# Four edits to the small matmuls of a hybrid mLSTM and sparse-attention layer on one core: compression operands laid out by offset, a zero-padded gather, and broadcasts in another form

## The chip, the core and the metric

One core of one Trainium2 chip runs the whole layer in one launch. The metric is the device time of that launch in microseconds (us). The engines are TensorE (PE in the rows, with PEld for its weight loads), VectorE (DVE), ScalarE (ACT), GpSimd (POOL) and SyncE (SP), which issues the DMAs. Each engine works through its own instructions in order, and semaphores tie the engines together.

## The reference, cut to what matters

```python
D_MODEL, SEQ = 2048, 512
def reference(x, c, ...):
    mod = silu(c) @ w_ada + b_ada
    shift, scale, gate = split(mod, 3)
    h = rmsnorm(x, ln_g) * (1 + scale) + shift
    p = h @ w_in + b_in                      # one projection, split into 15 parts
    y_m = mlstm_group(...)                   # 4 heads of 256, chunked recurrence, gated by rows i and f
    y_n = nsa_group(...)                     # 16 query heads in 4 groups: compressed, selected and window attention
    y = concat([y_m, y_n]) @ w_out
    return rmsnorm(x + gate * y, final_g)
...
    # inside nsa_group: 31 blocks of 32 positions, at a stride of 16
    def compress(a, pos, w1, w2):
        blk = a[:, cidx] + pos
        return gelu(blk.reshape(..., CMP_LEN * dh) @ w1) @ w2
    k_cmp, v_cmp = compress(kc, ...), compress(vc, ...)
    p_c = masked_softmax(q @ k_cmp - slopes * distance)
    o_c = p_c @ v_cmp                        # the compressed branch, one of three that are gated and added
```

All tensors are float32. A product that has to keep that precision is made in one of two ways here: a plain float32 matmul, which the trace shows as two MATMUL records, or a split of an operand into a high and a low part in fp32r (hi/lo), with one record for each product of parts.

## The kernel before

The work is tiled to 128 partitions with the 512 positions along the free dimension. It runs through these stages.

Lines 155 to 277 normalise x, transpose it, compute shift and scale (`gemv`, float32 matmuls with 32 columns of weights at four column positions of the array, L203) and project the first seven column tiles (L256). Every later projection is `proj` (L279): two weight tiles of 128x1024 come by SP from DRAM into three rotating buffers (`raw`, L113), `split` (L119) makes a high part on ACT and a low part (names ending in `l`, L126) on DVE or POOL, and 48 matmuls of 512 columns add up one tile (L291 to L293). In the attention stage all low parts are made on POOL (L797).

Lines 345 to 413 compute the gate rows of the mLSTM. `gr` holds the projected rows, `fl` and `mr` are the results of two scans, and `rw` = `fl - mr` has four rows, one for each head. In each `memory_head` (L668) a matmul broadcasts one of these rows to 128 partitions: `rb` (L709), float32, four partitions deep, 512 columns.

`block_rows` (L418) writes the compression operand `cst` from a projection in PSUM. `compress` (L437) multiplies it with `w1`: 16 float32 matmuls of 124 columns for keys and 16 for values (`hid`, L444), each of which reads every eighth element of `cst`. The value result ends in `vcmp`, 32 partitions deep.

`attend` (L499) runs for 4 groups and 4 blocks of 128 queries. Its `gather` (L539) transposes the weights of four heads on PE, takes a high part on ACT (`ph`) and a low part on DVE (`pl`), and adds two matmuls of 512 columns into `o` (L548, L549). For the compressed branch these are 32 partitions deep (`phc`, `plc` with `vcmp`); for the others 128.

`gate_columns` (L778) runs as side work between the weight tiles of the mLSTM projections: 64 DMAs and 64 DVE operations make `gacc`, and 16 float32 matmuls of one column (`gcps`, L793) reduce it over partitions to the columns `gcol`. In the output stage `chunk_rows` (L833) broadcasts `gcol` into rows with 16 float32 matmuls of 128 columns (`gps`, L838); the products of the output projection are `po` (L899 to L901, and L908 to L910 for the last chunk).

The order on each engine comes from a scheduler that simulates the program, so a change of one operation can move others.

Of the kernel before, what the change touches and what calls it, by code (L numbers as in the profile page):

```python
# [86 lines left out]
def layer_kernel(ctx: ExitStack, tc: tile.TileContext, x, cols, ada, ada_g, w_ko, w_tiles,  # L87
# [221 lines left out]
    gr = const.tile([P, T], F32, name="gr")  # L309
    kcmp = const.tile([P, NG, 32], F32, name="kcmp")  # L310
    vcmp = const.tile([32, NG, P], F32R, name="vcmp")
# [14 lines left out]
    na = napool.__enter__()  # L326

# [54 lines left out]
    rw = gr[64:68, :]  # L382
# [10 lines left out]
    ve.tensor_sub(rw, fl, mr)  # L393
# [17 lines left out]
    for hd in range(MH):  # L411
# [5 lines left out]
            .rearrange("p (g t) -> p g t", g=NG) for vr in range(2)] for kv in range(2)]  # L417
    def block_rows(kv, ct2):  # L418
        nm = f"{'kv'[kv]}c{ct2}"
        ps = proj(nm)  # L420
        for gg in range(2):
            r = slice(64 * gg, 64 * gg + 64)
            pv = ps[r, :].rearrange("p (b l r) -> p b l r", l=8, r=2)
            for par in range(2):
                for vr in range(2):
                    po = COLS["pos"][0] + ((kv * 2 + par) * 2 + vr) * 8
                    ve.scalar_tensor_tensor(
                        cst[kv][vr][64 * par:64 * par + 64, 2 * ct2 + gg, :]
                        .rearrange("p (b l) -> p b l", l=8),
                        pv[:, :, :, par], bcol(nm)[r, :],  # L430
                        ct[r, po:po + 8].unsqueeze(1).to_broadcast([64, 32, 8]),
                        op0=ALU.add, op1=ALU.add)
# [3 lines left out]
                   zero[0:32, 0:1].to_broadcast([32, NG * P]))  # L436
    def compress(kv):  # L437

        hid = psb("ms", f"hid{kv}")
# [59 lines left out]
    def attend(g, qs, kh, kl, vt):  # L499
# [6 lines left out]
        for i in reversed(range(NT)):  # L506
# [161 lines left out]
    def memory_head(hd, vh, vl):  # L668
# [39 lines left out]
        dc = COLS["delta"][0] + hd * 16  # L708
        pe.matmul(rb, ct[64:68, dc:dc + 1].to_broadcast([4, P]), rw, start=True, stop=True)  # L709
# [68 lines left out]
    def gate_columns():  # L778
        for n in range(4):
            acc = na.tile([P, T], F32, tag="q", name=f"gacc{n}", bufs=QB)  # L780
            for k in range(KT):
# [12 lines left out]
            ve.tensor_add(gcol[:, 4 * n:4 * n + 4], ps[:, 0:4], col("b_agate", 4 * n, 4))  # L794
# [37 lines left out]
    wl_l = op.tile([P, KT, 256], F32R, name="wl_l")  # L832
    def chunk_rows(n, c0, cn):  # L833
# [195 lines left out]
```

## Time and profile before

| | |
|---|---|
| three timed runs | 1137.73, 1138.68 (median), 1139.94 us |
| the profiled execution | 1138.83 us, with a span of 1137.0 us |
| granted TensorE clock, mean | 0.996 |
| PE busy in the span | 1110.3 us, 98% |
| DVE, ACT, POOL busy | 668.1, 546.6 and 198.3 us |

The span runs from the first to the last instruction, and the 1.8 us around it are launch and end. A timeline row shows when an instruction starts and how long it is in flight. PE matmuls overlap, so what a matmul costs PE is the distance from its start to the next start, not its length.

### The profile page before, as it was taken

What the parts mean: (1) busy time and instruction counts of PE and PEld (TensorE: products, weight loads), DVE (VectorE), ACT (ScalarE), POOL (GpSimd) and SP (SyncE); (2) the same over time, 40 slices, a digit from 0 to 9 for tenths busy, and PEclk for the clock granted to TensorE, in tenths of its full rate; (3) what the DMA queues carried; (4) which work ended last, traced back from release to release, by engine and by line L of the source; (5) the groups of instructions that cost most, each with busy time, mean ns of one, the idle gap of its engine ahead of it and who ended that gap; (6) DMA issues with size and microseconds to landing.
All of it is one profiled execution on the core that took longest, in us unless ns stands there. A gap on an engine that the chain in (4) does not pass through costs nothing.

```text
span 1137.0 us, 18337 instructions
## 1 busy us (share of the span) xinstructions
PE 1110.3 (98%) x6796; PEld 919.1 (81%) x6796; DVE 668.1 (59%) x1712; ACT 546.6 (48%) x1222; POOL 198.3 (17%) x174
## 2 busy tenths in 40 slices
PE   4999999999999999999999999999999999999997
PEld 4777788887887888788788777888888888888896
DVE  5766464216647657666666885578567357334273
ACT  5443452237666758766756734333433354223242
POOL 1000200443335325333533210000000000000000
PEclk9999999999999999999999999999999999999999
DMA  9999423232111211121121442238416222444334
GB/s 378 406 402 363 146 93 130 93 112 74 56 56 59 72 56 56 62 68 57 61 70 57 138 158 77 91 134 290 151 57 214 84 91 75 148 140 133 104 114 158
DMA packets 49338, 150.29 MB, mean 132 GB/s; under 512 B 5856, under 2 KB 7776, under 8 KB 48736
## 3 DMA queue, kind: packets, MB, share of 16 engines
q1 hardware_dynamic: 49248, 149.12, 37.7%
q8 instruction: 53, 0.87, 0.3%
q14 instruction: 37, 0.30, 0.1%
HBM read 144.90 MB, written 4.19 MB: 131 GB/s over the span
## 4 chain that ended last, share of the span: by engine, by line
PE 93%; DVE 2%; DMA 2%; ACT 1%; issue 0%; POOL 0%; SPq 0%; ACTq 0%; POOLq 0%; DVEq 0%
PE ko L256 7%; PE po L899 5%; PE po L900 5%; PE po L901 5%; PE pj_q L291 3%; PE pj_mz L291 3%; PE pj_mx L291 3%; PE pj_mz L292 3%; PE pj_mv L291 3%; PE pj_q L292 3%; PE pj_mz L293 3%; PE pj_q L293 3%; PE pj_mx L292 3%; PE pj_mv L293 3%; PE pj_mv L292 3%; PE pj_mx L293 3%
## 5 line engine op out<-in xcount | busy, mean ns | idle before, releaser
L524 ACT ACTIVATE ep<-ep,nm 128x512 f32<-128x512 f32 (+3 forms) x128 | 71.3, 558 | 19.3 <-DVE nm L517 18.6
L749 POOL TENSOR_TENSOR sm<-sm,mhalf 128x1 f32<-128x1 f32 x16 | 10.1, 640 | 254.5 <-DVE sm L748 113.1
L788 DVE SCALAR_TENSOR_TENSOR gacc<-adag,sil,gacc 128x512 f32<-128x512 f32 x60 | 48.0, 801 | 7.5 <-DMA adag<-in_dram 6.9
L517 DVE CUSTOM_DVE_ANT_0 ep<-ss,bias 128x512 f32<-128x512 f32 (+3 forms) x64 | 30.3, 486 | 30.7 <-PE tps L543 22.1
L517 DVE CUSTOM_DVE_ANT_0 ep<-sw,bias 128x512 f32<-128x512 f32 (+3 forms) x64 | 29.9, 484 | 18.9 <-PE sw L585 12.9
L194 DVE SCALAR_TENSOR_TENSOR acc<-ada,sil,acc 128x256 f32<-128x256 f32 x75 | 35.7, 476 | 1.5
L220 ACT ACTIVATE hhi<-xts,md 128x512 fp32r<-128x512 f32 x16 | 13.1, 817 | 47.3 <-DVE md L210 47.3
L537 DVE TENSOR_SCALAR ep<-ep,ff 128x512 f32<-128x512 f32 (+3 forms) x80 | 33.2, 461 | 0.6
L861 POOL TENSOR_TENSOR rf<-rf,mhalf 128x1 f32<-128x1 f32 x4 | 2.2, 549 | 178.7 <-ACT tz L854 163.1
L547 DVE TENSOR_TENSOR pls<-tps,phs 128x512 fp32r<-128x512 f32 x40 | 27.0, 685 | 10.6 <-ACT phs L546 10.1
L547 DVE TENSOR_TENSOR plw<-tpw,phw 128x512 fp32r<-128x512 f32 x40 | 27.2, 684 | 6.7 <-ACT phw L546 6.1
L504 POOL TENSOR_SCALAR bias<-ct 128x640 f32<-128x640 f32 x16 | 29.4, 1839 | 2.3 <-DVE nm L517 1.2
L546 ACT CAST phw<-tpw 128x512 fp32r<-128x512 f32 x40 | 22.8, 583 | 13.3 <-PE tpw L543 8.4
L524 ACT ACTIVATE ec<-ec,nm 128x32 f32<-128x32 f32 x64 | 20.3, 317 | 17.6 <-DVE nm L517 17.2
L546 ACT CAST phs<-tps 128x512 fp32r<-128x512 f32 x40 | 23.0, 582 | 11.2 <-DVE nm L517 5.0
L203 PEld LDWEIGHTS gp<-ada,cb 128*32 128x32 f32 x1328 | 20.5, 112 | 8.9 <-issue 6.8
L543 PE MATMUL tpw<-ct,ep 128*128 128x128 f32 x160 | 26.8, 273 | 0.1
L517 DVE CUSTOM_DVE_ANT_0 ec<-ss,bias 128x32 f32<-128x32 f32 x48 | 8.9, 187 | 29.1 <-PE ss L575 28.8
L535 ACT ACTIVATE ep<-ep,ff 128x512 f32<-128x512 f32 (+3 forms) x48 | 23.5, 552 | 4.4 <-DVE ff L529 4.3
L232 PE MATMUL xt<-ct,xs 128*128 128x128 f32 x64 | 11.0, 330 | 14.3 <-DVE xs L169 12.4
L203 PE MATMUL gp<-ada,cb 128*32 128x64 f32 x1328 | 24.9, 224 | 0.0
L543 PE MATMUL tps<-ct,ep 128*128 128x128 f32 x160 | 24.8, 272 | 0.0
(1084 smaller groups left out, 3831.4 us busy)
## 6 DMA issues: line engine op xcount, KB each, us to landing
ada<-in_dram SPq DMA_DIRECT2D x64, 512.0 KB, 7.0
adag<-in_dram SPq DMA_DIRECT2D x64, 256.0 KB, 3.7
wo<-in_dram SPq DMA_DIRECT2D x32, 512.0 KB, 3.4
w_q<-in_dram SPq DMA_DIRECT2D x16, 512.0 KB, 3.5
w_mx<-in_dram SPq DMA_DIRECT2D x16, 512.0 KB, 3.4
w_mv<-in_dram SPq DMA_DIRECT2D x16, 512.0 KB, 3.4
w_mz<-in_dram SPq DMA_DIRECT2D x16, 512.0 KB, 3.5
w_mo<-in_dram SPq DMA_DIRECT2D x16, 512.0 KB, 3.4
```

The lines of the kernel that those rows point to most:

```text
L256: pe.matmul(ko_ps[j], (wl if p == 1 else wh)[:, c], (hlo if p == 2 else hhi)[k], start=(k == 0 and p == 0), stop=(k == KT - 1 and p == 2))
L291: pe.matmul(ps, wh[:, c], hhi[k], start=(k == 0), stop=False)
L292: pe.matmul(ps, wh[:, c], hlo[k], start=False, stop=False)
L293: pe.matmul(ps, wl[:, c], hhi[k], start=False, stop=(k == KT - 1))
L517: ve.tensor_tensor_reduce(dst, src, bs, -0.125, 3.0e38, ALU.add, ALU.min, nm[:, c:c + 1])
L524: sc.activation(tiles[hd], tiles[hd], AF.Exp, bias=nm[:, 4 * br + hd:4 * br + hd + 1], scale=-1.0, accum_out=zz[:, 4 * br + hd:4 * br + hd ...
L543: pe.transpose(tp[0:rows, hd * P:(hd + 1) * P], srcs[hd], ident)
L547: ve.tensor_sub(pl[0:rows, :], tp[0:rows, :], ph[0:rows, :].bitcast(F32))
L788: ve.scalar_tensor_tensor(acc, raw, w, acc, op0=ALU.mult, op1=ALU.add)
L899: pe.matmul(pss[i][:, :cn], yh[k][:, t], wh[:, c], start=f0, stop=False)
L900: pe.matmul(pss[i][:, :cn], yh[k][:, t], wl[:, c], start=False, stop=False)
L901: pe.matmul(pss[i][:, :cn], yl[k][:, t], wh[:, c], start=False, stop=l0)
```

## The change

There are five edits.

1. `cst` is laid out with the offset `l` first, so that `hid` reads 127 elements in a row (the columns between groups are computed and not used) in place of 4 x 31 elements at a stride of eight. `block_rows` writes with the inverse stride.
2. `vcmp` and the compressed `ph` become 128 partitions deep: high part in rows 0 to 31, low part in rows 32 to 63, zeros below, which POOL writes by a memset in every gather. One matmul takes the place of two.
3. `rw` becomes an fp32r tile of 128 partitions with high rows, low rows and zeros, and `dsel` a selector of the same depth; `rb` is one fp32r matmul. To build them there are new operations on DVE, ACT and POOL and three small DMAs on SP.
4. `gcps` uses 32 columns of ones as weights at four column positions, with 128 columns of `gacc` moving, and a DVE transpose follows.
5. `gps` is made from `gcol` in high and low parts: DVE multiplies the identity with them into `dg`, and two fp32r matmuls per chunk add the two.

```diff
-    gr = const.tile([P, T], F32, name="gr")
+    rw = const.tile([P, T], F32R, name="rw")
+    dsel = const.tile([P, 64], F32R, name="dsel")
-    vcmp = const.tile([32, NG, P], F32R, name="vcmp")
+    vcmp = const.tile([P, NG, P], F32R, name="vcmp")
...
-    ve.tensor_sub(rw, fl, mr)
+    gp.memset(rs, 0.0)
+    gp.memset(ds, 0.0)
+    for r in range(2):
+        nc.sync.dma_start(ds[4 * r:4 * r + 4, :], cols[0:4, COLS["delta"][0]:COLS["delta"][0] + 64])
+    ve.tensor_copy(dsel, ds)
+    ve.tensor_sub(rd, fl, mr)
+    sc.copy(rh, rd)
+    ve.tensor_copy(rs[0:4, :], rh.bitcast(F32))
+    ve.tensor_sub(rd, rd, rh.bitcast(F32))
+    nc.sync.dma_start(rs[4:8, :], rd)
+    sc.copy(rw, rs)
...
-                        cst[kv][vr][64 * par:64 * par + 64, 2 * ct2 + gg, :]
-                        .rearrange("p (b l) -> p b l", l=8),
+                        cst[kv][vr][64 * par:64 * par + 64, :, (2 * ct2 + gg) * 32:(2 * ct2 + gg + 1) * 32]
+                        .rearrange("p l b -> p b l"),
...
-                pe.matmul(hid[:, 0:NG * NCMP], raw[:, l * P:(l + 1) * P],
-                          cst[kv][half].rearrange("p g (b l) -> p g b l", l=8)
-                          [:, :, half:half + NCMP, l],
+                pe.matmul(hid[:, 0:nb], raw[:, l * P:(l + 1) * P], cst[kv][half][:, l, half:half + nb],
...
+                if rows == 32:
+                    gp.memset(ph[64:128, :].bitcast(F32), 0.0)
+                    sc.copy(ph[0:32, :], tp[0:32, :])
+                    ve.tensor_sub(ph[32:64, :], tp[0:32, :], ph[0:32, :].bitcast(F32))
+                    pe.matmul(ops, vmat, ph, start=first[0], stop=last)
+                    first[0] = False
+                    return
...
-        pe.matmul(rb, ct[64:68, dc:dc + 1].to_broadcast([4, P]), rw, start=True, stop=True)
+        pe.matmul(rb, dsel[:, hd * 16:hd * 16 + 1].to_broadcast([P, P]), rw, start=True, stop=True)
...
-            for j in range(4):
-                pe.matmul(ps[:, j:j + 1], acc[:, j * P:(j + 1) * P], ones[:, 0:1], start=True, stop=True)
+            for g in range(4):
+                pe.matmul(ps[32 * g:32 * g + 32, 0:P].rearrange("p (j c) -> p j c", j=4), ones[:, 0:32],
+                          acc.rearrange("p (j c) -> p j c", j=4)[:, :, 32 * g:32 * g + 32],
+                          start=True, stop=True, tile_position=(0, 32 * g))
+            tr = tmp(f"gtr{n}", P)
+            ve.transpose(tr, ps[:, 0:P])
...
-        for j in range(cn // P):
-            k = c0 // P + j
-            pe.matmul(ps[:, j * P:(j + 1) * P], gcol[:, k:k + 1].to_broadcast([P, P]), ident,
-                      start=True, stop=True)
+        for v, gc in enumerate((gch, gcl)):
+            dg = op.tile([P, 4, P], F32R, tag="dg", name=f"dg{n}{v}", bufs=2)
+            ve.tensor_mul(dg[:, 0:m], ident.unsqueeze(1).to_broadcast([P, m, P]),
+                          gc[:, c0 // P:c0 // P + m].bitcast(F32).unsqueeze(2).to_broadcast([P, m, P]))
+            pe.matmul(ps[:, :cn], onr, dg[:, 0:m].rearrange("p a b -> p (a b)"), start=(v == 0), stop=(v == 1))
```

At three places the order of instructions matters for what follows. On DVE, where the gate rows are computed, before the change:

```order
L394 TENSOR_TENSOR zt<-gr,fl 4x512
L405 TENSOR_TENSOR gpr<-gpr,fl 4x1 x3
L393 TENSOR_TENSOR gr<-fl,mr 4x512
L405 TENSOR_TENSOR gpr<-gpr,fl 4x1 x2
L126 TENSOR_TENSOR w_kc_10l<-w_kc_1_2226,w_kc_10h 128x512
L405 TENSOR_TENSOR gpr<-gpr,fl 4x1
L407 TENSOR_TENSOR gpx<-gpr,ct 4x64
```

The row `gr<-fl,mr` is `rw`; eight writes of `cst` and then the low part `w_kc_11l` follow behind `gpx`. The same place on DVE after the change:

```order
L411 TENSOR_TENSOR zt<-gr,fl 4x512
L422 TENSOR_TENSOR gpr<-gpr,fl 4x1 x3
L405 TENSOR_TENSOR rd<-fl,mr 4x512
L422 TENSOR_TENSOR gpr<-gpr,fl 4x1 x2
L126 TENSOR_TENSOR w_kc_10l<-w_kc_1_2242,w_kc_10h 128x512
L422 TENSOR_TENSOR gpr<-gpr,fl 4x1
L407 COPY rs<-rh 4x512
L408 TENSOR_TENSOR rd<-rd,rh 4x512
L424 TENSOR_TENSOR gpx<-gpr,ct 4x64
```

Two operations, `rs<-rh` and `rd<-rd,rh`, now stand ahead of `gpx`, of the `cst` writes and of `w_kc_11l`.

On POOL in the attention stage (group 1), before, the low parts of the projection weights stand in a row:

```order
L126 TENSOR_TENSOR w_v_01l<-w_v_0_5346,w_v_01h 128x512
L126 TENSOR_TENSOR w_v_10l<-w_v_1_5380,w_v_10h 128x512
L126 TENSOR_TENSOR w_v_11l<-w_v_1_5380,w_v_11h 128x512
L126 TENSOR_TENSOR w_q_0_00l<-w_q_0_0_5426,w_q_0_00h 128x512
L126 TENSOR_TENSOR w_q_0_01l<-w_q_0_0_5426,w_q_0_01h 128x512
```

and after:

```order
L126 TENSOR_TENSOR w_v_01l<-w_v_0_5352,w_v_01h 128x512
L126 TENSOR_TENSOR w_v_10l<-w_v_1_5386,w_v_10h 128x512
L564 MEMSET phc_4008 64x512
L126 TENSOR_TENSOR w_v_11l<-w_v_1_5386,w_v_11h 128x512
L126 TENSOR_TENSOR w_q_0_00l<-w_q_0_0_5432,w_q_0_00h 128x512
```

The memset of the padded `ph` now stands ahead of `w_v_11l`; it waits until PE has read what the buffer held. There are 16 such memsets.

On PE at the start of the output stage, before:

```order
L292 MATMUL pj_mo_9648<-hhi_1863,w_mo_11h 128x512
L293 MATMUL pj_mo_9648<-hhi_1863,w_mo_11l 128x512
L838 MATMUL gps_9799<-ct,gcol 128x128 x4
L899 MATMUL po_9808<-wo000h,yh_9723 128x512
L900 MATMUL po_9808<-wo000l,yh_9723 128x512
```

and after, 107 rows further on:

```order
L938 MATMUL po_9827<-wo040h,yh_9765 128x512
L939 MATMUL po_9827<-wo040l,yh_9765 128x512
L878 MATMUL gps_9815<-dg_9816,onr 128x512
L940 MATMUL po_9827<-wo040h,yl_9766 128x512
L938 MATMUL po_9828<-wo040h,yh_9765 128x512
L878 MATMUL gps_9815<-dg_9819,onr 128x512
```

The broadcast of the first chunk moved from ahead of the first output product to the products of the fifth weight tile.

## Rows read from the trace of the kernel before

**Rows 1.** The page: busy time by engine, and the chain by engine
```profile
PE 1110.3 (98%) x6796; PEld 919.1 (81%) x6796; DVE 668.1 (59%) x1712; ACT 546.6 (48%) x1222; POOL 198.3 (17%) x174
...
PE 93%; DVE 2%; DMA 2%; ACT 1%; issue 0%; POOL 0%; SPq 0%; ACTq 0%; POOLq 0%; DVEq 0%
```

**Rows 2.** Windows: length; PE, PEld, DVE, ACT, POOL busy (instructions); clock; DMA share; GB/s
```profile
620.00:640.00 20.00, 18.88 (x99) 15.59 (x98) 12.08 (x58) 15.32 (x50) 2.58 (x2) 0.93 0.35 107
640.00:660.00 20.00, 20.00 (x97) 15.98 (x96) 19.00 (x32) 11.71 (x28) 10.14 (x7) 0.98 0.57 180
660.00:680.00 20.00, 18.38 (x95) 14.97 (x94) 17.84 (x42) 9.06 (x20) 1.91 (x2) 1.00 0.50 160
```

**Rows 3.** PE timeline at key compression: start, length, engine, line, operation, shape, count
```profile
185.21 7.37 PE L444 MATMUL hid<-cst,w 128*128 128x124 f32 x32
192.22 0.60 PE L291 MATMUL pj_vc<-hhi,w_vc_00h 128*128 128x512 f32 x1
192.66 0.39 PE L292 MATMUL pj_vc<-hlo,w_vc_00h 128*128 128x512 f32 x1
```

**Rows 4.** PE timeline around one compressed gather
```profile
364.18 0.40 PE L291 MATMUL pj_q<-hhi,w_q_10h 128*128 128x512 f32 x1
364.41 0.40 PE L292 MATMUL pj_q<-hlo,w_q_10h 128*128 128x512 f32 x1
364.74 0.50 PE L548 MATMUL o<-phc,vcmp 32*128 32x512 f32 x1
365.08 0.39 PE L549 MATMUL o<-plc,vcmp 32*128 32x512 f32 x1
365.40 0.50 PE L548 MATMUL o<-phs,v 128*128 128x512 f32 x1
365.74 0.39 PE L549 MATMUL o<-pls,v 128*128 128x512 f32 x1
```

**Rows 5.** PE timeline at the row broadcast of one mLSTM head
```profile
810.03 1.12 PE L709 MATMUL rb<-gr,ct 4*128 4x512 f32 x2
811.08 0.51 PE L702 MATMUL qk<-xh,ah 128*128 128x512 f32 x1
```

**Rows 6.** PE timeline at one set of gate columns
```profile
785.32 0.95 PE L793 MATMUL gcps<-ones,gacc 128*128 128x1 f32 x8
786.13 0.47 PE L291 MATMUL pj_mz<-hhi,w_mz_00h 128*128 128x512 f32 x1
```

**Rows 7.** PE timeline at the gate rows of the first output chunk
```profile
947.10 1.05 PE L838 MATMUL gps<-ct,gcol 128*128 128x128 f32 x8
947.90 0.48 PE L899 MATMUL po<-wo000h,yh 128*128 128x512 f32 x1
948.22 0.39 PE L900 MATMUL po<-wo000l,yh 128*128 128x512 f32 x1
```

**Rows 8.** PE timeline, matmuls with 32 weight columns in four column positions
```profile
41.78 1.32 PE L203 MATMUL gp<-ada,cb 128*32 128x64 f32 x80
42.92 0.29 PE L203 MATMUL gp<-acc,ones 128*32 128x64 f32 x8
43.15 1.20 PE L256 MATMUL ko<-hhi,ko_0h 128*128 128x512 f32 x4
44.18 0.39 PE L256 MATMUL ko<-hhi,ko_4h 128*128 128x512 f32 x1
```

**Rows 9.** DVE timeline where the compression operand is written
```profile
165.87 3.56 DVE L427 SCALAR_TENSOR_TENSOR cst<-pj_kc,ct 64x256 f32<-64x256 f32 x8
169.46 0.69 DVE L126 TENSOR_TENSOR w_kc_11l<-w_kc,w_kc_11h 128x512 fp32r<-128x512 f32 x1
```

**Rows 10.** PE timeline, the first use of that low part
```profile
171.91 0.50 PE L293 MATMUL pj_kc<-hhi,w_kc_11l 128*128 128x512 f32 x1
```

**Rows 11.** SP timeline, the issue of the first compression weights
```profile
170.18 1.98 SPq L442 DMA_DIRECT2D w<-in_dram  x2
```

**Rows 12.** POOL by form: line, operation, tile, shape, count, busy us, mean ns
```profile
L383 POOL MEMSET zt<- 64x512 f32 x1 | 0.5, 517 | 0.0
```

**Rows 13.** POOL timeline, a low part in the attention stage
```profile
376.64 1.29 POOL L126 TENSOR_TENSOR w_q_11l<-w_q,w_q_11h 128x512 fp32r<-128x512 f32 x1 [2.72 <-ACT w_q_11h L123]
```

**Rows 14.** PE timeline, its first use
```profile
385.88 0.39 PE L293 MATMUL pj_q<-hhi,w_q_11l 128*128 128x512 f32 x1
```

More of the change, by code (lines that the diff above doesn't have):

```diff
@@ L326, in layer_kernel @@
     na = napool.__enter__()
+    gr = na.tile([P, T], F32, tag="q", name="gr", bufs=QB)
     def tmp(name, n=T):
@@ L381, in layer_kernel @@
     zt = na.tile([P, T], F32, tag="q", name="zt", bufs=NB["q"])[0:64, :]
-    rw = gr[64:68, :]
     gp.memset(zt, 0.0)
@@ L392, in layer_kernel @@
     ve.tensor_tensor_scan(mr, fr, gr[0:4, :], 0.0, ALU.add, ALU.max)
-    ve.tensor_sub(rw, fl, mr)
+    rd = na.tile([P, T], F32, tag="q", name="rd", bufs=QB)[0:4, :]
+    rh = na.tile([P, T], F32R, tag="q", name="rh", bufs=QB)[0:4, :]
+    rs = na.tile([P, T], F32, tag="q", name="rs", bufs=QB)
+    ds = na.tile([P, T], F32, tag="q", name="ds", bufs=QB)[:, 0:64]
+    gp.memset(rs, 0.0)
[9 more added lines that the diff above has]
+    sc.copy(rw, rs)
     ve.tensor_sub(zt[0:4, :], gr[0:4, :], fl)
@@ L416, in layer_kernel @@
     cst = [[na.tile([P, 1056], F32, tag=("kh", "kl")[vr], name=f"cst{kv}{vr}", bufs=2)[:, :1024]
-            .rearrange("p (g t) -> p g t", g=NG) for vr in range(2)] for kv in range(2)]
+            .rearrange("p (l x) -> p l x", l=8) for vr in range(2)] for kv in range(2)]
     def block_rows(kv, ct2):
@@ L435, in layer_kernel @@
     ve.tensor_copy(vcmp.rearrange("p g c -> p (g c)"),
-                   zero[0:32, 0:1].to_broadcast([32, NG * P]))
+                   zero[:, 0:1].to_broadcast([P, NG * P]))
     def compress(kv):
+        nb = NG * 32 - 1
         hid = psb("ms", f"hid{kv}")
@@ L443, in compress @@
             for l in range(8):
-                pe.matmul(hid[:, 0:NG * NCMP], raw[:, l * P:(l + 1) * P],
-                          cst[kv][half].rearrange("p g (b l) -> p g b l", l=8)
-                          [:, :, half:half + NCMP, l],
+                pe.matmul(hid[:, 0:nb], raw[:, l * P:(l + 1) * P], cst[kv][half][:, l, half:half + nb],
                           start=(half == 0 and l == 0), stop=(half == 1 and l == 7))
-        hs = na.tile([P, NG * NCMP], F32, tag="hs", name=f"hs{kv}", bufs=1)
-        sc.activation(hs, hid[:, 0:NG * NCMP], AF.Gelu_apprx_tanh)
+        hs = tmp(f"hs{kv}", nb)
+        sc.activation(hs, hid[:, 0:nb], AF.Gelu_apprx_tanh)
         if kv == 0:
             kc = psb("ms", "kcps")
-            pe.matmul(kc[:, 0:NG * NCMP], w2s[:, 0:128], hs, start=True, stop=True)
+            pe.matmul(kc[:, 0:nb], w2s[:, 0:128], hs, start=True, stop=True)
             ve.tensor_copy(kcmp[:, :, 0:NCMP],
-                           kc[:, 0:NG * NCMP].rearrange("p (g b) -> p g b", b=NCMP))
+                           kc[:, 0:NG * 32].rearrange("p (g b) -> p g b", b=32)[:, :, 0:NCMP])
         else:
@@ L457, in compress @@
             for g in range(NG):
-                pe.matmul(vc[0:NCMP, g * DH:(g + 1) * DH], hs[:, g * NCMP:(g + 1) * NCMP],
+                pe.matmul(vc[0:NCMP, g * DH:(g + 1) * DH], hs[:, g * 32:g * 32 + NCMP],
                           w2s[:, 128:192], start=True, stop=True)
             vv = vc[0:NCMP, 0:NG * DH].rearrange("p (g d) -> p g d", d=DH)
-            sc.copy(vcmp[0:NCMP, :, 0:DH], vv)
-            ve.tensor_sub(vcmp[0:NCMP, :, DH:P], vv, vcmp[0:NCMP, :, 0:DH].bitcast(F32))
+            for r in (0, 32):
+                sc.copy(vcmp[r:r + NCMP, :, 0:DH], vv)
+            for r in (0, 32):
+                ve.tensor_sub(vcmp[r:r + NCMP, :, DH:P], vv, vcmp[0:NCMP, :, 0:DH].bitcast(F32))
     block_rows(0, 0)
@@ L791, in gate_columns @@
             ps = psb("ms", f"gcps{n}")
-            for j in range(4):
-                pe.matmul(ps[:, j:j + 1], acc[:, j * P:(j + 1) * P], ones[:, 0:1], start=True, stop=True)
-            ve.tensor_add(gcol[:, 4 * n:4 * n + 4], ps[:, 0:4], col("b_agate", 4 * n, 4))
+            for g in range(4):
[4 more added lines that the diff above has]
+            ve.transpose(tr, ps[:, 0:P])
+            ve.tensor_add(gcol[:, 4 * n:4 * n + 4], tr.rearrange("p (j c) -> p j c", j=4)[:, :, 0],
+                          col("b_agate", 4 * n, 4))
             yield
@@ L832, in layer_kernel @@
     wl_l = op.tile([P, KT, 256], F32R, name="wl_l")
+    gch = op.tile([P, KT], F32R, name="gch")
+    gcl = op.tile([P, KT], F32R, name="gcl")
+    onr = op.tile([P, P], F32R, name="onr")
+    sc.copy(gch, gcol)
+    ve.tensor_sub(gcl, gcol, gch.bitcast(F32))
+    sc.copy(onr, ones)
     def chunk_rows(n, c0, cn):
         ps = psb("ms", f"gps{n}")
-        for j in range(cn // P):
-            k = c0 // P + j
-            pe.matmul(ps[:, j * P:(j + 1) * P], gcol[:, k:k + 1].to_broadcast([P, P]), ident,
-                      start=True, stop=True)
+        m = cn // P
+        for v, gc in enumerate((gch, gcl)):
[3 more added lines that the diff above has]
+            pe.matmul(ps[:, :cn], onr, dg[:, 0:m].rearrange("p a b -> p (a b)"), start=(v == 0), stop=(v == 1))
         gb = op.tile([P, 512], F32, tag="gb", name=f"gb{n}", bufs=2)
```

1 line of the change is left out of this document (removed).

## The prediction

> **What bounds the kernel now.** I read the page first: PE is busy for 98% of the span, and PE holds 93% of the chain that ended last [rows 1]. Busy time alone proves little, because matmuls overlap, so I went through the PE timeline from start to start. In the projections a 512-column matmul starts 0.23 us after the one before it (364.18 to 364.41), although it is in flight for 0.40 us [rows 4]. That pace holds nearly everywhere. The one stretch behind the first 20 us where PE stands idle is at 620 to 680 us: 1.1 us and 1.6 us are missing in two windows, DVE is busy for 19.0 of 20 us between them, and the granted clock falls to 0.93 in the first [rows 2]. So a microsecond of PE's pace that is removed should come off the end, except in that stretch, where DVE sets the pace. All terms are made against the profiled execution, 1138.83 us, which is 0.15 us above the median.
>
> **Compression operand by offset (edit 1).** The 32 records of `hid` run from 185.21 to 192.22, and the next matmul needs 0.44 us instead of 0.23: 7.01 + 0.21 = 7.22 us, or 0.22 us a record [rows 3]. The float32 matmuls of `gps` have as many weights and 128 columns in place of 124, but read them in a row, and eight of them take 0.80 us plus 0.32 - 0.23 = 0.09 us at the next matmul: 0.11 us a record [rows 7]. Hence 32 records of 127 columns should take 3.6 us. The difference is 3.6 us, twice (keys and values): **7.2 us**. With 0.10 us a record it is 7.9.
>
> The writes of `cst` get the inverse stride. Eight of them take 3.56 us and `w_kc_11l` waits behind them until 170.15 [rows 9]; PE uses it at 171.91 [rows 10], a slack of 1.76 us. Edit 3 puts two operations of 4x512 ahead of them; a two-input operation of 128x512 takes 0.69 us [rows 9], so they cost 1.4 us at most, and I take 1.0. That leaves 0.76 us, so nothing is late if the stride of a write is free. No row shows a write with such a stride; if it doubled the writes, 3.56 - 0.76 = 2.8 us would be PE's wait. A gain is excluded, because PE doesn't wait there now. I take nothing, as the read side of these same writes is strided already, and keep 2.8 for the range.
>
> **Padded gather (edit 2).** Around a compressed gather the distances are 0.33 (the matmul before), 0.34 (`phc`), 0.32 (`plc`) and 0.34 (`phs`), and then 0.23 again [rows 4]. Against the pace of 0.23 that is 0.10 + 0.34 + 0.32 + 0.11 = 0.87 us. I read this as a price of changing the depth from 128 partitions to 32 and back, and of being 32 deep, because the pair behind it, 128 deep and with as many columns, has only the 0.34 at the change. After the edit one matmul of 128 partitions stands there: 0.23 us. That is 0.64 us for each of 16 gathers: **10.2 us**. Two of the 16 lie in the stretch that DVE paces [rows 2], and I count them as lost: 1.3 us back.
>
> The Trainium skill speaks against most of this: "TensorE: Matmul & The Clock Gate", section "Why this matters for your kernels", says that a single matmul of K=32 takes the same time as one of K=128. By it only one of two equal matmuls would go, 16 x 0.23 = 3.7 us. The trace disagrees: 0.32 and 0.34 us at 32 partitions against 0.23 at 128 [rows 4].
>
> The memset that the padding needs goes to POOL. One of this size takes 0.52 us [rows 12], so 16 are 8 us on an engine that is busy for 198 [rows 1]. What stands behind it is a low part of the weights, which ends at 377.93 in the tightest case of the 84 in this stage [rows 13] and is first used at 385.88 [rows 14]: 7.95 us of lead covers the memset. If that cover were gone, each would cost up to 1.8 us.
>
> **Row broadcasts (edit 3).** `rb` takes 1.05 us [rows 5], and with the changes of depth before and behind it, 0.10 and 0.11 as at the gather [rows 4], 1.26 us. One fp32r matmul of 512 columns and 128 partitions takes 0.23. So 1.03 us, four times: **4.1 us**. The way to the new operand is hidden: on SP the DMA of the low rows waits for DVE at about 167 us (the `cst` writes behind it start at 165.87 now, plus the 1.0 [rows 9]), and the next issue behind it, of `w1`, comes at 170.18 now [rows 11]. On ACT the copy of `rw` waits for that DMA with the high parts of the next tile behind it, which PE wants ten matmuls after 171.91, at 174.3 [rows 10]. A landing of up to 5 us fits in; a slower one would cost the difference, at most 2 us. The three DMAs are small, and I take nothing.
>
> **Gate columns (edit 4).** Eight records of `gcps` take 0.81 us [rows 6], with 0.09 behind them as at `gps` 0.90, and four sets are 3.6 us. After it, column positions: 80 records of 64 columns take 1.14 us, so 0.014 each, and a record of 128 columns 0.029. The eight records that follow take 0.23, which is 0.12 over their work, and the first four `ko` behind them 1.03 instead of 0.92 [rows 8]. With 0.10 for the entry a set would cost 0.23 + 0.12 + 0.11 + 0.10 = 0.56 us. In the new order two of the sets are cut in two by the transposes of `ht`, and two positions at a time take as long as four, so these two cost 1.1 each: 3.3 us in all. The gain is **0.3 us**, between a loss of 0.8 (all four cut) and a gain of 1.7 (no entry price and none cut).
>
> **Gate rows (edit 5).** The five sets of `gps` are three of 0.89 and two of half that: 3.6 us [rows 7]. After it come six matmuls of 512 columns and four of 256: 6 x 0.23 + 4 x 0.12 = 1.9. The gain is **1.7 us**. The ten products `dg`, 0.69 us each at most [rows 9], stand on DVE behind the low parts of the fifth weight tile, and only the end of the chunk needs them. With no time between the fifth tile and the chunk's end they would cost 7 us, but three weight tiles lie in between.
>
> **The sum.** 7.2 + 10.2 + 4.1 + 0.3 + 1.7 = 23.5, less 1.3 in the stretch of DVE: 22.2 us. 1138.83 - 22.2 = **1116.6 us**.
>
> **The rivals.**
> - *The stride is not what slows `hid`.* Then 7.2 us stay: 1123.8. For it: 0.22 us is the very pace of a 512-column matmul, which could be chance. Against it: `gps` with the same weights runs at half the time [rows 3, 7]. 5 in 100.
> - *Depth is not what slows the gather.* If the price is that of `vcmp` itself, one matmul of 0.32 goes, 5.1 us instead of 10.2: 1121.7. By the skill's rule it is 3.7 us and 1123.1. Against both: `rb`, four deep, shows the same step at the next matmul, 0.34 [rows 4, 5]. 6 in 100 for the two.
> - *The strided writes of `cst` are slow.* 2.8 us of wait at 171.9: 1119.4. 8 in 100.
> - *Slower than before.* POOL becomes PE's bound in the attention stage. The memset waits until PE has read the old `ph`, a low part waits behind the memset, and PE waits for that low part: 0.52 + 1.29 [rows 12, 13], 1.8 us for each of 16 gathers, 29 us: 1145.6. It decides once POOL starts a memset so late that 7.95 - 1.8 = 6.1 us of the lead are used up. For it: the order puts each memset ahead of a low part. Against it: the scheduler placed it where the old reader should be done. 3 in 100.
>
> **How the numbers follow.** The forecast has 78 in 100. Its own span is 1112.3 (nothing lost to DVE, 1.3; edit 4 at its best, 1.4; `hid` at 0.10 us a record, 0.7; about 1 us of the idle in rows 2 gone) to 1121 (the DMA's 2, edit 4 at its worst, 1.1, and that idle half as much again, 1.3). The range takes in the first three rivals and leaves out the fourth: 1112.3 to 1124. Comparing runs tells apart about 0.2% here, 2.3 us. All cases but the last are faster by more: faster 0.96, the same 0.01, slower 0.03.
>
> **What would show it.** `hid` in about 3.6 us twice; one `o<-phc` of 128 partitions with 0.23 us to the next start; `rb` at 0.23; `gcps` at 0.5 to 1.1 a set; two `gps` matmuls inside the chunk; PE still without idle time at 171 us and from 260 to 620. The forecast is wrong if PE shows new waits for POOL, or for DVE's `w_kc_11l`, or if the idle stretch at 620 to 680 grows by more than it is now.

## The result: 12 us faster, 10 us less than forecast

| | before | after |
|---|---|---|
| timed runs, median | 1139.2 us (1137.73 to 1139.94) | 1127.07 us (1126.6 to 1127.6) |
| the profiled execution, span | 1137.0 us | 1125.8 us |
| PE busy | 1110.3 us | 1092.4 us |
| DVE busy | 668.1 us | 693.0 us |

The ratio is 0.9895, with a 95% interval of 0.9878 to 0.9912. The change is faster, by 12.1 us (1.1%); the forecast was 22.2 us, and the time lies outside its range. Each edit's matmuls, taken by themselves, became cheaper by about what was worked out. The waits between the matmuls grew, because one of the edits brought a new order of the instructions.

### The profile after

The page: busy time by engine, and the chain by engine (before: [rows 1]).

```profile
PE 1092.4 (97%) x6754; PEld 908.2 (81%) x6754; DVE 693.0 (62%) x1731; ACT 548.3 (49%) x1227; POOL 206.8 (18%) x192
...
PE 92%; DVE 3%; ACT 2%; DMA 2%; issue 1%; POOL 0%; SPq 0%; ACTq 0%; POOLq 0%; DVEq 0%
```

PE is busy for 17.9 us less, but the span is only 11.2 us shorter. The difference is idle time of PE.

The PE timeline of the changed kernel at the five edits: start, length in flight, engine, line, operation, shape, count, and in brackets the idle time before it and what ended it.

```profile
172.07 0.50 PE L293 MATMUL pj_kc<-hhi,w_kc_11l 128*128 128x512 f32 x1 [0.16 <-DVE w_kc_11l L126]
...
185.72 3.73 PE L462 MATMUL hid<-cst,w 128*128 128x127 f32 x32
189.21 0.48 PE L291 MATMUL pj_vc<-hhi,w_vc_00h 128*128 128x512 f32 x1
...
357.28 0.39 PE L567 MATMUL o<-phc,vcmp 128*128 128x512 f32 x1
357.51 0.39 PE L573 MATMUL o<-phs,v 128*128 128x512 f32 x1
...
548.26 0.39 PE L733 MATMUL rb<-rw,dsel 128*128 128x512 f32 x1
548.50 0.39 PE L567 MATMUL o<-phc,vcmp 128*128 128x512 f32 x1
...
776.57 0.43 PE L818 MATMUL gcps<-gacc,ones 128*32 128x128 f32 x8
776.92 0.50 PE L291 MATMUL pj_mz<-hhi,w_mz_00h 128*128 128x512 f32 x1
...
800.72 0.39 PE L733 MATMUL rb<-rw,dsel 128*128 128x512 f32 x1
801.57 0.51 PE L727 MATMUL qk<-xh,ah 128*128 128x512 f32 x1 [0.46 <-ACT ah L720]
...
961.68 0.39 PE L878 MATMUL gps<-dg,onr 128*128 128x512 f32 x1
961.90 0.40 PE L940 MATMUL po<-wo040h,yl 128*128 128x512 f32 x1
```

Read from start to start, `hid` takes 3.49 us where it took 7.01 [rows 3], the padded gather 0.23 where the pair took 0.66 and its neighbours 0.21 more [rows 4], and a `gps` matmul 0.22 [rows 7]. In eight of the 16 gathers the padded matmul takes 0.31 to 0.32, because it stands right behind transposes; in seven of these the last transpose takes only 0.03, where it took 0.20 ahead of an old pair, so the saving is about the same. A whole set of `gcps` takes 0.35 [rows 6]. `rb` takes 0.24 in two heads, but in two others the next start comes after 0.85 us: PE stands there for 0.46 us until ScalarE has made `ah`.

The windows that answer to [rows 2]: length; PE, PEld, DVE, ACT, POOL busy (instructions); clock; DMA share; GB/s.

```profile
620.00:640.00 20.00, 16.34 (x72) 12.54 (x71) 19.31 (x57) 16.36 (x50) 6.55 (x5) 0.83 0.48 146
640.00:660.00 20.00, 17.73 (x89) 14.78 (x88) 17.25 (x31) 8.46 (x19) 5.33 (x4) 0.94 0.57 182
660.00:680.00 20.00, 20.00 (x101) 16.80 (x101) 14.09 (x45) 7.00 (x13) 2.19 (x4) 0.98 0.25 82
```

The 60 us hold 5.9 us without PE work where there were 2.7 [rows 2], and the granted clock is 0.83 in the first window. More than half of the missing gain went here. What PE waited for behind the start (in total, times, longest):

```profile
PE o L573 <- ACT phw L571: 2.6, 2, 2.2
PE h L763 <- DVE p1l L754: 2.0, 1, 2.0
...
PE pj_mo L293 <- POOL w_mo_00l L126: 1.2, 1, 1.2
PE o L574 <- DVE plw L572: 1.0, 1, 1.0
```

The waits of the first 35 us, for `xs`, `xts` and others, are left out; they are as long in the kernel before. All four shown are new or longer than before, where the longest wait behind 35 us was 0.9 us.

A measure that also catches the half clock is the **excess**: for each record of a matmul on PE, its distance to the next start less the median distance of its shape, summed where that is over 0.15 us. From 20 us to the end it is 9.1 us before and 22.1 us after, so 13.0 us more. The terms of the forecast sum to 23.5 us, and 23.5 - 13.0 = 10.5 us is within 0.7 us of what the profiled execution gained. By place, the excess is 4.6 us before and 11.8 after at 610 to 680 us; 0 and 1.8 at 420 to 460; 0 and 2.1 at 540 to 560. All three lie where an attention group ends.

The largest wait, on PE of the changed kernel:

```profile
623.12 0.60 PE L561 MATMUL tpw<-ct,ep 128*128 128x128 f32 x4
...
625.46 0.60 PE L561 MATMUL tpc<-ct,ec 128*32 128x128 f32 x4
628.28 0.50 PE L573 MATMUL o<-phw,v 128*128 128x512 f32 x1 [2.22 <-ACT phw L571]
...
631.23 0.79 PE L293 MATMUL pj_mo<-hhi,w_mo_00l 128*128 128x512 f32 x1 [1.22 <-POOL w_mo_00l L126]
631.82 0.63 PE L291 MATMUL pj_mo<-hhi,w_mo_00h 128*128 128x512 f32 x1
```

and on ScalarE, between those transposes and that product:

```profile
624.07 0.68 ACT L669 ACTIVATE ym<-pj_mz,ct 128x512 f32<-128x512 f32 x1
...
625.78 0.69 ACT L671 ACTIVATE th<-pj_mz,bhalf 128x512 f32<-128x512 f32 x1
...
627.64 0.59 ACT L571 CAST phw<-tpw 128x512 fp32r<-128x512 f32 x1
```

`tpw` is ready at 623.7 us. Its high part `phw` stands behind four activations of the second mLSTM head (two `ym`, two `th`) and a few shorter operations and starts at 627.64; PE, which has the product of `phw` next in its order, waits. The same place in the kernel before:

```profile
640.40 0.75 PE L543 MATMUL tpw<-ct,ep 128*128 128x128 f32 x4
...
645.38 0.39 PE L548 MATMUL o<-phw,v 128*128 128x512 f32 x1
```

There the transposes stand later and the product later still, with two `qk`, four `tpc` and 14 projection matmuls between; 5.0 us pass and nothing waits. After the wait the clock drops. Two windows of the changed kernel, columns as above:

```profile
625.50:631.20 5.70, 2.29 (x10) 1.03 (x8) 5.70 (x15) 5.70 (x16) 1.84 (x2) 0.91 0.44 121
631.20:636.90 5.70, 5.67 (x15) 4.54 (x16) 5.64 (x9) 3.23 (x11) 2.90 (x2) 0.50 0.48 168
```

PE was busy for 2.29 of 5.7 us, and the granted clock of the next 5.7 us is 0.50, the 1.2 GHz level. A 512-column matmul then starts every 0.43 us (631.82 to 632.25) instead of 0.23, so these waits cost more than their length. I estimate 2.7 us on top here, 0.20 of every 0.43 us over the 5.7 us.

### The profile page after: what moved, and what is told of

It reads as the page before. It is cut to its first block, busy times and chain, and to the rows that moved or that the text cites. A ratio compares the mean times of both kernels' runs of the same rounds, so it can differ in the third digit from the quotient of the medians.

```text
span 1125.8 us, 18318 instructions
## 1 busy us (share of the span) xinstructions
PE 1092.4 (97%) x6754; PEld 908.2 (81%) x6754; DVE 693.0 (62%) x1731; ACT 548.3 (49%) x1227; POOL 206.8 (18%) x192
## 4 chain that ended last, share of the span: by engine, by line
PE 92%; DVE 3%; ACT 2%; DMA 2%; issue 1%; POOL 0%; SPq 0%; ACTq 0%; POOLq 0%; DVEq 0%
PE ko L256 7%; PE po L938 5%; PE po L939 5%; PE po L940 5%; PE pj_mx L291 3%; PE pj_mx L292 3%; PE pj_mv L293 3%; PE pj_mx L293 3%; PE pj_mv L291 3%; PE pj_mv L292 3%; PE pj_q L291 3%; PE pj_mz L291 3%; PE pj_q L293 3%; PE pj_q L292 3%; PE pj_mz L292 3%; PE pj_mz L293 2%
## 5 line engine op out<-in xcount | busy, mean ns | idle before, releaser
L555 DVE TENSOR_SCALAR ep<-ep,ff 128x512 f32<-128x512 f32 (+3 forms) x80 | 36.8, 509 | 0.6
L553 ACT ACTIVATE ep<-ep,ff 128x512 f32<-128x512 f32 (+3 forms) x48 | 23.7, 555 | 7.9 <-DVE ff L547 7.6
L561 PEld LDWEIGHTS tps<-ct,ep 128*128 128x128 f32 x160 | 20.4, 142 | 5.9 <-DVE ep L555 0.7
L232 PE MATMUL xt<-ct,xs 128*128 128x128 f32 x64 | 10.8, 327 | 14.4 <-DVE xs L169 12.5
```

## The experiments

Two theories came first. **A**: edit 2 brought a new order of the instructions, and the new waits belong to that order. **B**: VectorE and ScalarE set the pace at 620 to 660 us whatever the order, and PE time taken away ahead of that stretch is given back in it. For single waits, **C** says that one queue's order makes them and **D** that the engines there are too full.

### Each edit alone

Four kernels, each the kernel before with a part of the diff that stands ahead of the prediction.

e1_offset_only has edit 1:

```diff
-                          [:, :, half:half + NCMP, l],
+                pe.matmul(hid[:, 0:nb], raw[:, l * P:(l + 1) * P], cst[kv][half][:, l, half:half + nb],
```

> The kernel before with edit 1 alone (compression operand by offset). Both theories give hid its 2 x 3.6 us on TensorE. Theory A (the gather's edit rearranged the queues of the attention stage, and the new waits at 430, 550 and 625 to 660 us belong to that order): the order of this kernel hardly differs from that of before, so the whole 7.2 us reaches the end, 1131 to 1132 us, and the stretch at 620 to 660 loses about 3 us in waits, as before. Theory B (in the stretch at 620 to 660 VectorE and ScalarE set the pace whatever the order, and TensorE time taken away ahead of it is given back there): 1 to 3 us of gain, 1136 to 1138 us, with longer waits at 620 to 660.

e2_gather_only has edit 2:

```diff
+                    gp.memset(ph[64:128, :].bitcast(F32), 0.0)
+                    pe.matmul(ops, vmat, ph, start=first[0], stop=last)
```

> The kernel before with edit 2 alone (padded gather). The compressed gathers cost TensorE 10.2 us less by the forecast. Theory A: this edit brings the new order with its waits, so of the 10.2 us only 0 to 3 are left, 1136 to 1139 us, with waits of 2 us and more between 620 and 660. Theory B: the 14 gathers ahead of the stretch give their 9 us back there as every other gain does, and edits 1 and 2 look alike: 1136 to 1138 us. Had the forecast been right for this edit, 1130 us.

e3_rb_only has edit 3:

```diff
-        pe.matmul(rb, ct[64:68, dc:dc + 1].to_broadcast([4, P]), rw, start=True, stop=True)
+        pe.matmul(rb, dsel[:, hd * 16:hd * 16 + 1].to_broadcast([P, P]), rw, start=True, stop=True)
```

> The kernel before with edit 3 alone (row broadcasts). Forecast for it 4.1 us, 1134.6 us. In the changed kernel two of the four rb are followed by 0.3 us of waiting for the high part ah on ScalarE, and the low part w_kc_11l comes 0.6 us late, so theory A gives 2.9 us: 1135.5 to 1136.5. Theory B gives the same for three of the four broadcasts, which come behind the stretch, and loses the first: 1136 to 1137.

e4_gates_only has edits 4 and 5:

```diff
-                pe.matmul(ps[:, j:j + 1], acc[:, j * P:(j + 1) * P], ones[:, 0:1], start=True, stop=True)
+            for g in range(4):
+                pe.matmul(ps[32 * g:32 * g + 32, 0:P].rearrange("p (j c) -> p j c", j=4), ones[:, 0:32],
...
+            pe.matmul(ps[:, :cn], onr, dg[:, 0:m].rearrange("p a b -> p (a b)"), start=(v == 0), stop=(v == 1))
```

> The kernel before with edits 4 and 5 alone (gate columns and gate rows). Forecast 0.3 + 1.7 us, and both come behind 660 us, so both theories let them reach the end: 1136.5 to 1137.2 us. If the writes of dg on VectorE delay the first output chunk, the gain is 1 us smaller.

The kernel before took 1139.03 us beside them.

| | measured | gain | ratio, 95% interval | forecast | PE records that moved, of 6796 |
|---|---|---|---|---|---|
| e1, edit 1 | 1132.32 us | 6.7 us | 0.9938, 0.9924 to 0.9953 | 7.2 us | 0 |
| e2, edit 2 | 1137.25 us | 1.8 us | 0.9987, 0.9978 to 0.9997 | 8.9 us | 649 |
| e3, edit 3 | 1135.97 us | 3.1 us | 0.9973, 0.9963 to 0.9983 | 4.1 us | 9 |
| e4, edits 4 and 5 | 1136.79 us | 2.2 us | 0.9978, 0.9969 to 0.9987 | 2.0 us | 22 |

The last column counts the records that have to change place to turn PE's order in the kernel before into the new one, without those that the edit itself replaces. The three kernels that keep the order have nearly their forecast, and edit 1, whose matmuls lie ahead of the stretch at 620, brings its 6.7 us through it: theory B falls. Edit 2 moved a tenth of PE's records and kept 1.8 us of 10.2. Its waits are those of the changed kernel: 2.2 us for `phw`, 1.7 for `p1l`, 0.8 for `w_mo_00l`.

### Single causes in the changed kernel

f1_phw_first sets one place of ScalarE's order right: the activations `ym` and `th` of the second head are queued behind the `phw` that PE waited for.

```diff
+                phi[nme] = sc.copy(ph[0:rows, :], tp[0:rows, :]).ins
...
+            with tc.issue_after(phi["w311"]) if hd == 1 else nullcontext():
+                sc.activation(ym[i], ps, AF.Identity, bias=bcol(nm))
+                sc.activation(th, ps, AF.Tanh, bias=bhalf[:, TIDX[nm]:TIDX[nm] + 1], scale=0.5)
```

> The changed kernel (1127.1 us), with one order put right: on ScalarE the four activations ym and th of the second mLSTM head are queued behind the last high part phw that attention block 1 of group 3 needs, for which TensorE waited 2.2 us at 626 to 628. Theory C (the wait is the order of ScalarE's queue): that wait goes, and with it part of the half clock that followed, some 13 matmuls at 0.43 us instead of 0.23, or 2.6 us: 1122 to 1125 us. Theory D (VectorE and ScalarE are too full between 620 and 660 whatever stands first): the wait turns up again behind the next low part, plw, al or w_mo_00l, and the time stays at 1126 to 1128.

f2_columns_later starts the side work one head later in the changed kernel, and f3_before_columns_later does the same in the kernel before.

```diff
         if hd == 0:
             pat[0] = "v"
+        if hd == 1:
             side_work.append(gate_columns())
```

> The changed kernel with the gate columns (64 operations of 0.75 us on VectorE and their 64 loads) begun one mLSTM head later, so that VectorE has nothing of them between 620 and 660. Theory D: TensorE's excess of 11.3 us in that stretch falls to 5 or less, 1120 to 1123 us. Theory C: ScalarE's order there is the same, so the wait of 2.2 us for phw and the half clock behind it stay, and only the wait of 2.0 us for p1l at 655 goes: 1125. If the columns get ready late for the output stage, 1 to 3 us come back there.

> The kernel before (1139.0 us) with the same shift of the gate columns, to see what the shift does without the change. Its excess between 620 and 680 is 5.5 us. Theory D: 3 to 5 us faster, 1134 to 1136. Theory C: 1 to 2 us, 1137 to 1138.

f4_gather_64_deep takes the padding of the changed kernel away.

```diff
-                    gp.memset(ph[64:128, :].bitcast(F32), 0.0)
...
-                    pe.matmul(ops, vmat, ph, start=first[0], stop=last)
+                    pe.matmul(ops, vmat[0:64], ph[0:64, :], start=first[0], stop=last)
```

> The changed kernel with the padding taken away again: the compressed gather is one matmul of 64 partitions, high rows and low rows without zeros, and no memset on GpSimd. If a change of depth costs TensorE 0.10 and 0.11 us at any depth below 128, as the forecast read it, 16 gathers cost 3.4 us more: 1130 to 1131 us, with the waits of 430, 550 and 620 to 660 as in the changed kernel. If only the 32-deep form is slow, or if the memsets made the waits, 1127 or less; without the memset's waits 1117 to 1120.

**f1** took 1124.13 us (ratio to before 0.9869, 0.9852 to 0.9885; before 1139.37), 3 us better than the change. PE's timeline shows that the wait only moved one product on:

```profile
627.26 0.50 PE L575 MATMUL o<-phw,v 128*128 128x512 f32 x1
629.71 0.50 PE L576 MATMUL o<-plw,v 128*128 128x512 f32 x1 [1.95 <-DVE plw L574]
```

and VectorE's why:

```profile
628.25 0.74 DVE L815 SCALAR_TENSOR_TENSOR gacc<-adag,sil,gacc 128x512 f32<-128x512 f32 x1
...
629.00 0.66 DVE L574 TENSOR_TENSOR plw<-tpw,phw 128x512 fp32r<-128x512 f32 x1
```

The low part `plw` stands behind a step of the gate columns, and that behind a low part `xl`. Both theories are half right: the time is that of C, the moved wait that of D. One repair on one queue didn't cure this order.

**f2** took 1121.47 us (0.9847, 0.9832 to 0.9862) and **f3** 1136.81 (0.998, 0.9971 to 0.999). The shift is worth 5.6 us in the changed kernel and 2.6 in the one before, so about 3 us of the missing gain go with VectorE's side work, which the new order meets harder; with intervals of 1 to 2 us on either side of each time this difference is near the edge of the noise. The windows of f2:

```profile
620.00:640.00 20.00, 17.46 (x87) 13.44 (x86) 18.10 (x58) 17.84 (x55) 6.56 (x6) 0.91 0.26 80
640.00:660.00 20.00, 20.00 (x105) 17.07 (x104) 13.62 (x37) 10.45 (x23) 6.34 (x6) 1.00 0.26 80
```

From 640 to 680 us PE is never idle, and the wait of 2.0 us for `p1l` is gone; the 2.2 us for `phw`, ahead of it, stay. Theory C foresaw both, but 1125 us; theory D foresaw the time (1120 to 1123) and nearly the excess (5 or less; it is 5.4 us at 610 to 680). So again each is half right. f3 lies between the two forecasts for it, 1134 to 1136 and 1137 to 1138.

**f4** took 1129.52 us (0.9919, 0.9904 to 0.9934), so the padding is worth 2.4 us. Its PE order is nearly that of the changed kernel (71 records moved, against some 670 from the kernel before) and its waits are at the same three places, without any memset: the memsets made neither. The price of depth was a miss:

```profile
272.13 0.39 PE L292 MATMUL pj_v<-hlo,w_v_10h 128*128 128x512 f32 x1
272.45 0.50 PE L566 MATMUL o<-phc,vcmp 64*128 64x512 f32 x1
272.88 0.51 PE L572 MATMUL o<-phs,v 128*128 128x512 f32 x1
273.22 0.60 PE L561 MATMUL tps<-ct,ep 128*128 128x128 f32 x4
```

The matmul that is 64 deep takes 0.43 us to the next start, the one ahead of it 0.32 and the one behind it 0.34. I had expected 0.23 for it and a price only at its neighbours. Against 0.23 for each of the three that is 0.40 us more than at 128, or some 6.3 us for 16 gathers. Of these 3.4 us took the place of waits (the excess is 18.7 us, against 22.1), so the span became only 2.9 us longer (1128.7 us against 1125.8).

### The same work in the other order

The last seven kernels hold engines to an order: the end of the program chains the instructions of each held engine, in the sequence of another kernel, with edges that only set the order of issue. What only one of the two kernels has is free.

```diff
+    keep_order(tc, ORDER)
...
+                i = found.get(f"I-{at + k}")
+                if i is None:
+                    continue
+                if last is not None:
+                    tc.add_manual_dep(i, last.name, dep, reason="order")
+                last = i
```

`ORDER` is a table of the instructions' numbers, one row for each held engine. What each kernel holds, and on which work, is in the table behind the expectations.

> Edit 2 alone (1137.2 us), but with every engine held to the order that the kernel before has; only the 16 second matmuls are gone and the new memsets and copies are free to stand where they fit. Theory A (the new order ate the gain of this edit): nearly the 10.2 us of the forecast come out, 1129 to 1131 us, and the waits at 440, 560 and 637 to 665 us are those of the kernel before. Theory B (the engines' load between 620 and 660 sets the pace whatever the order): 1135 to 1138 us, as without the old order.

> The converse: the kernel before, no edit at all, with every engine held to the order that edit 2 alone brought (the 16 second matmuls of the gathers stand beside the first). Theory A: the order costs 7 to 9 us by itself, 1146 to 1149 us. Theory B: 1138 to 1141 us, since the work is that of the kernel before.

> The changed kernel (1127.1 us), held to the order of the kernel before where the two have the same instructions. If the terms of the forecast were right and only the order was not foreseen, 1117 to 1120 us. If theory B, 1125 to 1128 us.

> The changed kernel with the gate columns begun one head later, held to the order of the kernel before with the same shift (1136.8 us). Both causes taken away: theory A and the crowding by the gate columns together give 1114 to 1117 us; the shift alone gave 1121.5. Theory B: no better than 1120.

> The changed kernel (1127.1 us) with TensorE alone held to the order of the kernel before; ScalarE, VectorE, GpSimd and the DMA queue are ordered anew around it. With all engines held it took 1119.3 us. If the place of TensorE's products is what counts (o from phw set right behind the transposes that it needs), 1118 to 1121 us. If the helpers' order counts (phw behind ym and th on ScalarE), 1124 to 1128 us.

> The changed kernel with ScalarE and VectorE alone held to the order of the kernel before, TensorE ordered anew. If the helpers' order counts, 1118 to 1121 us. If TensorE's own order counts, 1124 to 1128 us. Both at 1118 to 1121 would mean that either side is enough; both above 1123 that the two orders must fit each other.

> The changed kernel with the gate columns begun one head later and TensorE alone held to the order that the kernel before has with that shift. If the two causes, TensorE's order (1127.1 to 1117.2 us) and the gate columns beside the last attention blocks (1127.1 to 1121.5 us), are separate, 1112 to 1114 us. If the shift helps only where TensorE waits anyway, 1115 to 1117 us, like the kernel with every engine held and the shift (1115.8).

| | work | order held | measured | gain on before | ratio, 95% interval |
|---|---|---|---|---|---|
| h1 | edit 2 | that of before, all engines | 1129.63 us | 9.2 us | 0.992, 0.9905 to 0.9935 |
| h2 | before | that of e2, all engines | 1144.36 us | -5.6 us | 1.0047, 1.0032 to 1.0062 |
| h3 | all edits | that of before, all engines | 1119.26 us | 19.6 us | 0.9827, 0.981 to 0.9843 |
| i1 | all edits | that of before, PE alone | 1117.22 us | 22.1 us | 0.9808, 0.9793 to 0.9822 |
| i2 | all edits | that of before, ScalarE and VectorE | 1125.25 us | 14.1 us | 0.9882, 0.9865 to 0.9898 |
| h4 | all edits, columns later | that of f3, all engines | 1115.79 us | 23.0 us | 0.9795, 0.978 to 0.9809 |
| j1 | all edits, columns later | that of f3, PE alone | 1115.13 us | 23.7 us | 0.9803, 0.9779 to 0.9827 |

(Before: 1138.81 us beside h, 1139.34 beside i, 1138.78 beside j.)

h1 and h2 settle it. Edit 2 in the old order is worth 9.2 us instead of 1.8, and the kernel before, with no edit at all, loses 5.6 us in the new order; h3 and h4 lie inside what theory A gave for them. h2 lost less than the 7 to 9 us expected. Some of the cost may arise only where the new order and the shorter gathers meet, but h2's interval reaches to 7.1 us, so that is not shown. The waits of h2 are those of the changed kernel:

```profile
PE o L549 <- DVE plw L547: 2.5, 2, 1.5
PE o L548 <- ACT phw L546: 1.8, 1, 1.8
PE pj_mo L293 <- POOL w_mo_00l L126: 1.2, 1, 1.2
PE h L739 <- DVE p1l L730: 1.1, 1, 1.1
```

i1 and i2 ask whose order it is. With PE held, all five edits gain 22.1 us; with ScalarE and VectorE held, 14.1, and PE's order is then neither the old one nor the new. A held PE pulled the helpers along, though: in i1 only 25 of ScalarE's 1222 records and 65 of VectorE's 1712 stand elsewhere than in the kernel before, against 177 and 221 in the changed kernel. So PE's old order is enough to bring the gain back, and the helpers' old order alone is not. Whether PE's old order would do as well beside the helpers' new one is not shown. The windows of i1:

```profile
620.00:640.00 20.00, 17.95 (x90) 14.31 (x91) 19.16 (x43) 14.36 (x36) 10.63 (x8) 1.00 0.59 188
640.00:660.00 20.00, 19.44 (x101) 16.42 (x100) 19.02 (x41) 9.59 (x21) 2.91 (x2) 1.00 0.50 170
```

VectorE is as full as in the changed kernel (19.2 and 19.0 us of 20), yet PE works 3.3 us more in the two windows and keeps its full clock, and its excess at 610 to 680 us is 5.2 us, close to the 4.6 of the kernel before. h4 and j1 add the later gate columns and are the best versions, 23 us better than before and 11 to 12 better than the change. On top of the held order the later columns are worth 3.5 and 1.5 us, against 5.6 on the free one: the two causes overlap, and j1, expected at 1112 to 1114 or at 1115 to 1117, came out at the second (three of its four executions took 1114.9 to 1115.4 us, one 1119.9).

What stays open is why the scheduler, with 16 matmuls fewer, arrived at another order; its own reckoning is in no trace.

## Why the prediction was wrong

**What bounds the kernel.** "A microsecond of PE's pace that is removed should come off the end" holds while the order stands. It was wrong as a rule for this change, and this is the step that failed: the argument took PE's order as given. I read the new order only where an operation of the diff had been inserted or moved. On PE some 675 of 6796 records changed place, most of them in the attention stage, and the transition at 618 to 660 us was among them. The excess grew by 13.0 us, and with PE held to the old order the same work took 1117.2 us instead of 1127.1. The sign was there: rows 2 showed the one stretch without slack, and I didn't ask whether PE's rows in it still stood as far behind the helpers as before. All three signs of being wrong that the prediction named appeared: PE waits for POOL (1.2 us) and for `w_kc_11l` (0.2), and the idle time at 620 to 680 us grew from 2.7 to 5.9. PE also stood idle at 26 and 30 us (1.6 and 0.9 us), which the prediction passed over; it does so in both kernels.

That i1 meets the forecast of 22.2 us so closely is in part luck. Its excess is 2.7 us above that of the kernel before, of which 1.1 lie at 171 us and 1.2 at `rb`, while the 1.3 us that were taken back for the stretch of VectorE are hardly lost (0.6).

**The stretch that VectorE paces.** I took 1.3 us back for it, as if only the two gathers inside it could be lost. It took 7.2 us (excess 11.8 against 4.6 at 610 to 680 us), and the ends of two earlier groups 4.0 more, where [rows 2] had given no warning. i1 shows that VectorE's load alone was not what did it: the load is the same there and the excess is 5.2 us. The 1.3 us were a term of the wrong kind, a bound by load, where the rows at 623 to 628 us show a price set by how far PE's product stands behind the helpers that feed it.

**Edit 1** was right: 3.58 us for `hid` with the 0.09 more at the matmul behind it, twice, against 3.6. e1's 6.7 us, with an interval of 5.4 to 8.7, agree with 7.2. The writes of `cst` did cost something: eight of them take longer than before [rows 9].

```profile
166.54 4.75 DVE L444 SCALAR_TENSOR_TENSOR cst<-pj_kc,ct 64x256 f32<-64x256 f32 x8
171.32 0.69 DVE L126 TENSOR_TENSOR w_kc_11l<-w_kc,w_kc_11h 128x512 fp32r<-128x512 f32 x1
```

4.75 us against 3.56 is 0.59 a write instead of 0.45: the write stride is not free. The eight writes grew by 1.2 us, between nothing and the doubling by 3.6 that I had as the two ends. With edit 3's operations ahead of them `w_kc_11l` came 1.9 us later, 0.1 more than the slack of 1.76. PE was 0.1 us ahead of the old kernel before this place and is 0.5 us behind it at `hid` (185.72 against 185.21), so the term that I put at nothing cost 0.6 us here.

**Edit 2** was right in its matmuls: 10.2 us, of which h1 got 9.2 with an interval of 7.4 to 10.8. The reason given for it was only half right. I had read the 0.87 us of the old gather as a price of changing the depth and of being 32 deep. In the kernel before, the first gather's two matmuls stand apart, each alone between matmuls of 128 partitions:

```profile
277.66 0.39 PE L291 MATMUL pj_v<-hhi,w_v_10h 128*128 128x512 f32 x1
277.98 0.50 PE L548 MATMUL o<-phc,vcmp 32*128 32x512 f32 x1
278.40 0.50 PE L292 MATMUL pj_v<-hlo,w_v_10h 128*128 128x512 f32 x1
278.74 0.39 PE L293 MATMUL pj_v<-hhi,w_v_10l 128*128 128x512 f32 x1
```

From the start of the matmul ahead to the start behind the one that follows, 277.66 to 278.74, these three take 0.39 us more than three at 0.23. The pair of [rows 4] with its two neighbours (364.41 to 365.74) takes 0.41 us more than four at 0.23, and the one 64 deep in f4 with its neighbours 0.40. So the price that these rows show is about 0.4 us for each time PE goes to a smaller depth and back, whether one matmul or two stand there; a second matmul 32 deep adds no more than one of 128.

The page "TensorE: Matmul & The Clock Gate" of the Trainium skill, section "Why this matters for your kernels", holds that a single matmul of 32 rows takes as long as one of 128. The prediction estimated from it that only 3.7 us would go, and h1's 9.2 us exclude that sum. They don't refute that sentence of the Trainium skill: by the rows, 0.23 us for one matmul and 0.41 for the change of depth give the 0.64 us of the forecast as well.

The POOL rival did not come true, though PE waits for POOL now:

```profile
624.13 0.52 POOL L564 MEMSET phc<- 64x512 f32 x1 [11.20 <-DVE plw L572]
629.36 1.82 POOL L126 TENSOR_TENSOR w_mo_00l<-w_mo,w_mo_00h 128x512 fp32r<-128x512 f32 x1 [4.71 <-ACT w_mo_00h L123]
```

POOL stood idle for 4.7 us ahead of `w_mo_00l`, until ScalarE had made the high part; the memset had ended long before.

**Edit 3** was over by 1.0 us (e3: 3.1, with an interval of 1.9 to 4.2; the time alone doesn't show the miss, the rows do). Its matmul takes 0.23 us, but in two heads the old one had covered the making of `ah` on ScalarE. With the cover gone PE waits 0.46 us there, and 0.85 us pass from `rb` to the next start instead of 1.05. The step that failed here is that I priced a slow matmul as if nothing ran beside it.

**Edits 4 and 5** were right: 2.2 us against 2.0. A whole set of `gcps` takes 0.35 us and 0.2 at its two ends, the 0.56 of the forecast, and no wait for `dg` is among PE's. PE waits 0.5 us for `nw` ahead of the first output products, in e4 too, which the forecast didn't have.

## What to carry to other kernels

Where a scheduler sets the order, an edit that removes work can move everything: compare the whole order of the engine that bounds, and where it moved, treat the waits of that stretch as unknown rather than as they were. Test an edit with the order held before judging it; here the same work took 1127 us in the scheduler's new order and 1117 with PE held to the old one. Before pricing a slow operation at its whole length, ask what runs beside it and would be waited for once it is short.

## What the runs showed of the hardware that I had not expected

A float32r matmul of 512 columns that stands alone among matmuls of 128 partitions took 0.42 or 0.43 us to the next start when it was 32 deep (at 277.98 and 279.28 in the kernel before), the same when it was 64 deep (f4, all 16 of them), and 0.23 when it was 128 deep. With the 0.10 us or so at the matmul ahead and at the one behind, each change to a smaller depth and back cost about 0.40 us, and two matmuls 32 deep side by side cost 0.41 together [rows 4]. Padding with zeros to 128 was the cheapest of the three depths.

A VectorE write of 64x256 float32 at a stride of 128 elements took 0.59 us (eight in 4.75), against 0.45 us with the elements of a row side by side (eight in 3.56, [rows 9]); both read the same strided PSUM data. With edit 1 alone (e1) eight took 4.73.
